# A two-block transformer kernel: six first weight chunks on unnormalised x, w_out's first chunks in three steps, the last sum of squares later

## The chip, the cores and the metric

The kernel runs on one core of a Trainium2 chip. The metric is device time in microseconds (us) of one execution. Five engines take part, each with a queue of its own that it works off in order: TensorE (PE; its weight loads, PEld, overlap the products), VectorE (DVE), ScalarE (ACT), GpSimd (POOL) and SyncE (SP, which issues most transfers). They meet through semaphores alone.

## What is computed

Two blocks in a row on one sequence of 256 tokens and 1024 features. The part that matters here is the first block:

```python
hn = rms_norm(x, ln_g[l])
proj = jnp.einsum('bsd,dc->bsc', hn, w_in[l])
(qa, ka, va, ga, qb, kb, vb, gb, qc, kc, vc, gc, gate_logits) = jnp.split(proj, SPLIT_POINTS, axis=-1)
qa = rms_norm(qa.reshape(b, s, H_A, HEAD_DIM), g[0])
ka = rms_norm(ka.reshape(b, s, H_A, HEAD_DIM), g[1])
o_a = moba_attention(qa, ka, va.reshape(b, s, H_A, HEAD_DIM), rel_bias[OFF_A:OFF_A + H_A])
...
branches = jnp.stack([o_a.reshape(b, s, W_BR) * jax.nn.silu(ga), ...], axis=2)
br = jnp.einsum('bsiw,iwd->bsid', branches, w_branch[l])
merged = jnp.sum(gates * br, axis=2)
x = x + jnp.einsum('bsd,de->bse', merged, w_out[l])
```

The second block has its own norms, modulated by a vector that comes from `silu(c) @ w_ada`, a convolution, attention over selected keys, and a mixture of 64 experts behind a router.

## The kernel before, in words

**Layout and split numbers.** x lies feature by token in eight tiles of 128 features (index k). All products keep float32 accuracy with three products: an operand is split into a rounded high half (H, by a copy on ACT) and the rest (L, a subtraction on DVE), and H·H, H·L and L·H are summed. So a weight chunk of 1024 x 256 costs one transfer of 1 MB, one split on ACT (L249), one on DVE (L250) and 48 products of 256 columns on PE: 8 features x 2 halves x 3.

**The stream of weights.** `L1_ORDER` (L36) lists the chunks of layer 1 by name; w_out's four and the later weights follow. `ahead` (L265) fetches and splits the next chunk, `weight` (L269) hands one out, `early` (L274) calls `ahead` in the middle of a chunk. The five buffers "raw" serve as landing place and for low halves by turns, so chunk n + 3 can land only when PE has done its last product on chunk n's low half.

**The first chunks.** PE first multiplies unnormalised x (times ln_g, halves `xsH`, `xsL`) and the result is scaled by each token's reciprocal norm r when it is read out: `proj_raw` (L670). These raw chunks are 0, 1 and 2 (qa.0, ka.0, va.0). Meanwhile the squares are summed, r is the power -0.5 on POOL (L703), and PE broadcasts r over the partitions into `bc`, a PSUM tile (L708). Then for each feature DVE computes `hn` (L713, reads bc; four buffers), ACT `hH` (L714), DVE `hL` (L715). Those 24 instructions stand in one block in which the orders of ACT and DVE are as written. Chunk 3 (ga.0) and all others use hH and hL.

**The order of the rest.** In layer 1 the order of PE is as written; the other engines' queues are ordered by a planner that takes, of what is ready by its own estimate, what stands first in the program, and so also takes work that is written far behind. `slot` (L446) is called twice in each chunk from chunk 2 on, at its half and its end; `later(d, f)` puts work d slots on. The transposes of qa.0 (`fin`, L757) fall into slot 1, those of ka.0 into slot 3, a chunk's w_ada sum two slots behind it. PSUM has two banks for each name, taken in turn (`pst`, L301): under "O", the sums take the first bank, bc the second, qa.0's transposes the first again and ka.0's the second again.

**w_ada.** `ada_piece` (L609) loads 1/48 of w_ada (0.5 MB, two buffers) and sums its product with silu(c) on DVE (L620). Each chunk from 3 to 50 has one piece; silu(c) itself is computed behind the normalisation (L723 to L728).

**The end of layer 1.** The branch products (L861) make the merged tiles `mg`, two features at a time, with hH (L881) and hL (L882). `proj_fm_k` (L366) multiplies w_out's first two chunks in two steps: features 0 to 5 of both chunks, then 6 and 7. Behind each w_out chunk the new x is squared (`ss_add`, L326), and four small products sum the squares; those of the last chunk stand at the end of layer 1. Layer 2 begins with raw chunks (L1094); behind feature 5, `norm_mod` (L1063) calls `ss_bc` (L338), which computes r by an integer estimate and three rounds of Newton on DVE, in eleven small steps (`rsqrt`, L279), and broadcasts it (L344). `ss_bc` is called a second time ahead of the router.

Of the kernel before, what the change touches and what calls it, by code (L numbers as in the profile page):

```python
# [11 lines left out]
F32 = mybir.dt.float32  # L12
F32R = mybir.dt.float32r
I32 = mybir.dt.int32
AF = mybir.ActivationFunctionType
OP = mybir.AluOpType
# [19 lines left out]
L1_ORDER = """  # L36
qa.0 ka.0 va.0 ga.0 qa.1 ka.1 va.1 ga.1
kvc.0 qc.0 gc.0 qc.1 gc.1
# [33 lines left out]
ROPE_CI, REL_CI = 20, 2  # L72
ATTN_PT, ATTN_PV, ATTN_O, PTS_BUFS = {1: 3, 3: 4}, 2, 1, 6
STOP = False
RAW_BUFS = 5
WARM, START_PARTS = 12, ((0, 2), (2, 4), (4, 8))
RAW_BC, L2_KIWI, TM_K = 6, 0, (4, 6)
ADA_LAG, ADA_SKIP = 2, (0, 1, 2)
L2_LAG = {'qi': 3, 'q': 4, 'k': 3}
# [127 lines left out]
class Build:  # L207
# [70 lines left out]

    def rsqrt(self, src, n, mul, dst, e=None):  # L279
        nc = self.nc  # L280
        e = e or nc.vector
        v = self.tiny.tile([128, 16], F32, tag="rv", name="rv")[:, 0:n]
        y = self.tiny.tile([128, 16], F32, tag="ry", name="ry")[:, 0:n]
        t = self.tiny.tile([128, 16], F32, tag="rt", name="rt")[:, 0:n]
        e.tensor_scalar(v, src, mul, EPS, OP.mult, OP.add)
        e.tensor_scalar(y.bitcast(I32), v.bitcast(I32), -0.5, 0x5F3759DF, OP.mult, OP.add)
        if e is nc.vector:
            for it in range(3):
                o = dst if it == 2 else y
                e.tensor_tensor(t, y, v, OP.mult)  # L290
                e.scalar_tensor_tensor(t, t, -0.5, y, OP.mult, OP.mult)
                e.scalar_tensor_tensor(o, t, 1.5, y, OP.add, OP.mult)
        else:
            for it in range(3):
                o = dst if it == 2 else y
                e.tensor_tensor(t, y, v, OP.mult)
                e.tensor_tensor(t, t, y, OP.mult)
                e.tensor_scalar(t, t, -0.5, 1.5, OP.mult, OP.add)
                e.tensor_tensor(o, t, y, OP.mult)

    def pst(self, shape, tag):  # L301
# [36 lines left out]
    def ss_bc(self, ss):  # L338
        nc = self.nc
        r = self.tiny.tile([128, 4], F32, tag="rr", name="rr")  # L340
        self.rsqrt(ss.rearrange("p a b -> p (a b)"), 4, 1.0 / D, r)
        bc = self.pst([128, S], "O")
        for qt in range(2):
            nc.tensor.matmul(bc[:, 128 * qt:128 * qt + 128], r[:, 2 * qt:2 * qt + 1].to_broadcast([128, 128]),  # L344
                             self.vec("ident"))
        return r, bc
# [19 lines left out]
    def proj_fm_k(self, ws, xs, tags):  # L366

        nc = self.nc
        out = [self.pst([128, 2, S], tag) for tag in tags]
        for ks in (range(KD - 2), (KD - 2, KD - 1)):  # L370
            for ps, (wH, wL) in zip(out, ws):
                for t in range(2):
                    for k in ks:
                        c = k * 256 + 128 * t
                        xH, xL = xs(k)
                        first = k == 0 and t == 0
                        for a, b in ((wH, xH), (wH, xL), (wL, xH)):
                            nc.tensor.matmul(ps[:, t, :], a[:, c:c + 128], b, start=first, stop=k == KD - 1,
                                             skip_group_check=True)
                            first = False  # L380
        return out
# [78 lines left out]
    def attn(self, groups, load_tb, sinks, done):  # L460
# [7 lines left out]
        def qk(g):  # L468
# [24 lines left out]
            if g == G - 1:  # L493
# [4 lines left out]
                else:  # L498
                    self.later(1, lambda: [exps(1), total()])
                for g in range(G):  # L500
                    self.later(ATTN_PT[G] + g, lambda g=g: pt(g))
                    self.later(ATTN_PT[G] + g + ATTN_PV, lambda g=g: pv(g))
                self.later(ATTN_PT[G] + G - 1 + ATTN_PV + ATTN_O, turn)

# [60 lines left out]
    def run(self):  # L565
        tc, nc, a = self.tc, self.nc, self.a
        with ExitStack() as es:
# [25 lines left out]
            with ExitStack() as es1:  # L593
# [4 lines left out]
                with tc.manual_schedule(engines={mybir.EngineType.PE}):  # L598
                    self.layer1()
                if STOP:  # L600
                    return
                self.layer2()
# [20 lines left out]
    def layer1(self):  # L623
        tc, nc, a = self.tc, self.nc, self.a
        x, hH, hL = self.x, self.hH, self.hL
        self.ada_n = 0
        rr = self.s2("rel_a", shape=(128, 512))
        re = self.s2("rel_b", shape=(128, 512))
# [81 lines left out]
        proj_raw(first[1], 4, 8, *w)  # L710
        for k in range(KD):
            hn = self.wk([128, S], "hn", 4)
            nc.vector.scalar_tensor_tensor(hn, x[:, k, :], self.vec("ln_g")[:, k:k + 1], bc, OP.mult, OP.mult)  # L713
            i0 = nc.scalar.activation(hH[:, k, :], hn, AF.Copy)  # L714
            i1 = nc.vector.tensor_tensor(hL[:, k, :], hn, hH[:, k, :], OP.subtract)  # L715
        order.__exit__(None, None, None)
        self.hold = ()
        with tc.issue_after(self.last_load):
            nc.sync.dma_start(self.cmat, a["c_mat"])

        self.silc = self.wk([128, D], "silc", 1)
        th = self.wk([128, D], "ada", ADA_BUFS)
        with tc.issue_after(self.last_load):  # L723
            nc.sync.dma_start(self.silc, bass.AP(a["c_row"].tensor, a["c_row"].offset, [[0, 128], [1, D]]))
        with self.behind((i0.ins,)):
            nc.scalar.activation(th, self.silc, AF.Tanh, scale=0.5)
        with self.behind((i1.ins,)):
            nc.vector.scalar_tensor_tensor(self.silc, th, 1.0, self.silc, OP.add, OP.mult)  # L728
        nsink = self.small([128, 8], F32, "nsink")
        nc.vector.tensor_scalar(nsink, self.vec("sink"), -1.0, None, OP.mult)  # L730
# [55 lines left out]
        def chunk(name, c, ci):  # L786
            if ci < 2:
                self.later(2 * ci + 1, qk_chunk(name, c, first[ci], r))
                return
            wH, wL = self.weight()  # L790
            kind = name[:2]
            if ci == 2:
                ps = self.pst([128, 2, S], "mm")
                T[name, c] = self.s2(name)
                for h in range(2):
                    proj_raw(ps, 4 * h, 4 * h + 4, wH, wL)
                    self.slot()
                for t in range(2):
                    nc.scalar.activation(T[name, c][:, t, :], ps[:, t, :], AF.Copy, scale=r[:, 2 * t:2 * t + 1])
            elif kind in ("va", "vb"):  # L800
                ps = self.proj_tm(wH, wL, self.xs, self.slot)
# [111 lines left out]
        for ci, o in enumerate(L1_ORDER):  # L913
# [15 lines left out]
            if ci not in ADA_SKIP:  # L929
                self.ada_piece()  # L930
            if (name, c) in when:
                self.later(L1_QK if ci > 1 else L1_QK + 1, lambda a=when[name, c]: start(*a))
# [9 lines left out]
        for m in range(4):  # L942
# [7 lines left out]
            self.raw_split(m)  # L950
        while late:
            late.pop(0)()
        self.debug("x1", x.rearrange("p a b -> p (a b)"))
# [129 lines left out]
    def layer2(self):  # L1083
# [8 lines left out]
        raw = [[self.pst([128, S + 2], tag) for t in range(2)] for tag in ("mm", "S", "T")]  # L1092
        for k in range(KD):
            if k == RAW_BC:  # L1094
                h = self.norm_mod(self.ss1)
# [705 lines left out]
```

## Time and profile before

| | us |
|---|---|
| median of 3 runs | 1008.88 (1006.52 to 1009.64) |
| the profiled execution | 1009.1 |
| its span | 1007.1 |
| PE busy | 964.2 (96%) |
| PEld, weight loads | 886.5 (88%) |
| DVE busy | 813.1 (81%) |
| ACT busy | 599.3 (60%) |
| POOL busy | 162.8 (16%) |

The span runs from the first to the last instruction of the profile; 2.0 us of the execution lie around it. Matmuls are pipelined and their ends are modelled, so a busy PE isn't PE at its peak, and the granted clock of PE says how fast it was allowed to run (1.00 is 2.4 GHz, 0.50 is 1.2 GHz). A wait is put down to what released it. Spans on POOL are rough.

### The profile page before, as it was taken

The numbers are of one execution on the slowest core, as the hardware profiler recorded it, in microseconds if no ns is written. First come the engines' busy times: TensorE is split into PE (matmuls) and PEld (weight loads), VectorE is DVE, ScalarE is ACT, GpSimd is POOL, SyncE is SP. The second block draws the span as 40 slices with busy tenths as digits, with TensorE's granted clock in tenths as the row PEclk, the third lists the DMA queues.
The fourth block names the chain that finished last, engine by engine and source line by source line (L and its number), as shares of the span: only waits on it lengthen the run. The fifth ranks groups of instructions, "written<-read, shape, count | busy, mean of one in ns | idle before, by whom it ended". The sixth has DMA issues, their size and how long they took to land. (4 is left out here: it accounts for less than half of the span.)

```text
span 1007.1 us, 20285 instructions
## 1 busy us (share of the span) xinstructions
PE 964.2 (96%) x6666; PEld 886.5 (88%) x6666; DVE 813.1 (81%) x1500; ACT 599.3 (60%) x936; POOL 162.8 (16%) x109
## 2 busy tenths in 40 slices
PE   8799999999999998999989989999999999999996
PEld 7699989999999998999888977788888888888885
DVE  4757877877768668686876689799999999999995
ACT  5455564546545644454544434488787887877874
POOL 2311110111011000030210300012122121221221
PEclk8899999999999999999988989999999999999998
DMA  7366566676566656344331405288888888888984
GB/s 262 139 210 223 207 215 225 251 282 220 198 248 231 233 198 231 131 175 167 129 116 60 161 28 189 74 281 304 300 293 303 286 301 308 293 304 286 308 295 146
DMA packets 51208, 221.91 MB, mean 220 GB/s; under 512 B 5924, under 2 KB 6310, under 8 KB 41552
## 3 DMA queue, kind: packets, MB, share of 16 engines
q1 hardware_dynamic: 48960, 214.67, 60.5%
q0 software_dynamic: 1760, 5.42, 2.2%
q10 hardware_dynamic: 432, 1.05, 0.3%
q8 instruction: 38, 0.62, 0.2%
q14 instruction: 18, 0.15, 0.0%
HBM read 220.01 MB, written 1.11 MB: 220 GB/s over the span
## 5 line engine op out<-in xcount | busy, mean ns | idle before, releaser
L249 ACT ACTIVATE wh<-raw 128x2048 fp32r<-128x2048 f32 x75 | 143.4, 1914 | 110.3 <-DMA raw<-w_in 75.3
L250 DVE TENSOR_TENSOR raw<-raw,wh 128x2048 fp32r<-128x2048 f32 x75 | 171.5, 2287 | 16.2 <-ACT wh L249 15.8
L1542 ACT ACTIVATE wh<-raw 128x1024 fp32r<-128x1024 f32 x136 | 139.3, 1056 | 59.7 <-PE mm L1567 49.6
L350 PE MATMUL mm<-wh,hH 128*128 128x256 f32 x496 | 142.8, 288 | 0.5 <-DVE v L229 0.5
L351 PE MATMUL mm<-raw,hH 128*128 128x256 f32 x496 | 139.6, 281 | 0.2 <-DVE raw L250 0.2
L352 PE MATMUL mm<-wh,hL 128*128 128x256 f32 x496 | 139.6, 281 | 0.0
L1551 POOL TENSOR_TENSOR raw<-raw,wh 128x1024 fp32r<-128x1024 f32 x32 | 76.9, 2404 | 306.2 <-PE mm L1567 306.2
L350 PE MATMUL mm<-hH,wh 128*128 128x256 f32 x352 | 104.3, 296 | 2.0 <-ACT hH L714 2.0
L351 PE MATMUL mm<-hL,wh 128*128 128x256 f32 x352 | 101.3, 288 | 5.0 <-DVE hL L715 4.9
L1566 PE MATMUL mm<-wh,xH 128*128 128x512 f32 x264 | 106.1, 402 | 0.0
L1567 PE MATMUL mm<-wh,xL 128*128 128x512 f32 x264 | 103.4, 392 | 0.0
L352 PE MATMUL mm<-hH,raw 128*128 128x256 f32 x352 | 101.1, 287 | 1.6 <-DVE raw L250 1.6
L350 PEld LDWEIGHTS mm<-wh,hH 128*128 128x128 f32 x496 | 93.6, 189 | 2.2 <-DVE v L229 0.7
L351 PEld LDWEIGHTS mm<-raw,hH 128*128 128x128 f32 x496 | 93.6, 189 | 0.4 <-DVE raw L250 0.4
L352 PEld LDWEIGHTS mm<-wh,hL 128*128 128x128 f32 x496 | 93.6, 189 | 0.1
L620 DVE CUSTOM_DVE_ANT_0 ada<-ada,silc 128x1024 f32<-128x1024 f32 x48 | 58.6, 1221 | 31.8 <-DMA ada<-w_ada 31.6
L1545 DVE TENSOR_TENSOR raw<-raw,wh 128x1024 fp32r<-128x1024 f32 x68 | 79.8, 1210 | 0.0
L1545 DVE TENSOR_TENSOR WL<-raw,wh 128x1024 fp32r<-128x1024 f32 x66 | 79.8, 1210 | 0.0
L351 PEld LDWEIGHTS mm<-hL,wh 128*128 128x128 f32 x352 | 68.9, 196 | 5.8 <-DVE hL L715 5.8
L350 PEld LDWEIGHTS mm<-hH,wh 128*128 128x128 f32 x352 | 68.9, 196 | 3.5 <-ACT hH L714 2.7
L352 PEld LDWEIGHTS mm<-hH,raw 128*128 128x128 f32 x352 | 68.9, 196 | 1.8 <-DVE raw L250 1.8
L427 POOL TENSOR_TENSOR hr<-hss,mhalf 128x8 f32<-128x8 f32 (+2 forms) x24 | 44.2, 1844 | 158.7 <-DVE hss L426 158.5
(515 smaller groups left out, 2539.8 us busy)
## 6 DMA issues: line engine op xcount, KB each, us to landing
raw<-w SPq DMA_DIRECT2D x204, 512.0 KB, 5.3
raw<-w_in SPq DMA_DIRECT2D x58, 1024.0 KB, 4.8
ada<-w_ada SPq DMA_DIRECT2D x48, 512.0 KB, 5.7
raw<-w_out SPq DMA_DIRECT2D x8, 1024.0 KB, 4.8
raw<-w_branch SPq DMA_DIRECT2D x6, 1024.0 KB, 4.8
tb<-rext POOLq DMA_DIRECT2D x20, 256.0 KB, 5.0
raw<-ws SPq DMA_DIRECT2D x3, 1024.0 KB, 5.0
out<-x SPq DMA_DIRECT2D x4, 256.0 KB, 2.3
```

Of the source, the lines that this page charges most:

```text
L249: h = nc.scalar.activation(hi, raw, AF.Copy)
L250: l = nc.vector.tensor_tensor(lo, raw, hi, OP.subtract)
L350: nc.tensor.matmul(out, lh, rh, start=start, stop=False)
L351: nc.tensor.matmul(out, lh, rl, start=False, stop=False)
L352: self.last_mm = nc.tensor.matmul(out, ll, rh, start=False, stop=stop).ins
L427: nc.gpsimd.tensor_tensor(r, ss, self.mhalf[:, 0:2 * nh], OP.pow)
L620: nc.vector.tensor_tensor_reduce(raw, raw, self.silc, 0.5, 0.0, OP.mult, OP.add, self.ada[:, m:m + 1])
L1542: nc.scalar.activation(WH[h][:, half(p)], rw[h][:, half(p)], AF.Copy)
L1545: nc.vector.tensor_tensor(WL[h][:, half(p)], rw[h][:, half(p)], WH[h][:, half(p)], OP.subtract)
L1551: (nc.vector, nc.gpsimd)[f].tensor_tensor(VL[f], rw2[f], VH[f], OP.subtract)
L1566: nc.tensor.matmul(pa, xH[h][:, k, :], WH[h][:, ws], start=h == 0 and k == 0, stop=False)
L1567: nc.tensor.matmul(pa, xL[h][:, k, :], WH[h][:, ws], start=False, stop=False)
```

## The change

The order of the first eight chunks becomes qa.0, ka.0, va.0, qa.1, ka.1, va.1, ga.0, ga.1, and the first six are raw. The normalisation is cut into three pieces (features 0 to 2, 3 to 5, 6 and 7), written behind chunks 2, 3 and 4, without a fixed order of ACT and DVE; silu(c) comes behind chunk 5. The pieces of w_ada begin with chunk 5, and chunks 45 and 48 have two. w_out's first two chunks are multiplied in three steps. The last four sums of squares are written behind the third feature of layer 2's first chunks. `rsqrt` is gone; `ss_bc` computes r by one DVE step and a power on POOL. (The attention's lags move into a variable, with the same values; a switch that was off is removed.)

```diff
-qa.0 ka.0 va.0 ga.0 qa.1 ka.1 va.1 ga.1
+qa.0 ka.0 va.0 qa.1 ka.1 va.1 ga.0 ga.1
...
-ADA_LAG, ADA_SKIP = 2, (0, 1, 2)
+ADA_TWICE = (45, 48)
+ADA_LAG, ADA_SKIP, RAW_CHUNKS = 2, (0, 1, 2, 3, 4), 6
...
     def ss_bc(self, ss):
...
-        self.rsqrt(ss.rearrange("p a b -> p (a b)"), 4, 1.0 / D, r)
+        nc.vector.tensor_scalar(r, ss.rearrange("p a b -> p (a b)"), 1.0 / D, EPS, OP.mult, OP.add)
+        nc.gpsimd.tensor_tensor(r, r, self.mhalf[:, 0:4], OP.pow)
...
-        for ks in (range(KD - 2), (KD - 2, KD - 1)):
+        for ks in (range(4), (4, 5), (6, 7)):
...
-        for k in range(KD):
-            hn = self.wk([128, S], "hn", 4)
-            nc.vector.scalar_tensor_tensor(hn, x[:, k, :], self.vec("ln_g")[:, k:k + 1], bc, OP.mult, OP.mult)
-            i0 = nc.scalar.activation(hH[:, k, :], hn, AF.Copy)
-            i1 = nc.vector.tensor_tensor(hL[:, k, :], hn, hH[:, k, :], OP.subtract)
         order.__exit__(None, None, None)
...
+        def normalize(k0, k1):
+            for k in range(k0, k1):
+                hn = self.wk([128, S], "hn", 4)
+                nc.vector.scalar_tensor_tensor(hn, x[:, k, :], self.vec("ln_g")[:, k:k + 1], bc, OP.mult, OP.mult)
+                nc.scalar.activation(hH[:, k, :], hn, AF.Copy)
+                nc.vector.tensor_tensor(hL[:, k, :], hn, hH[:, k, :], OP.subtract)
+
+        def condition():
+            self.silc = self.wk([128, D], "silc", 1)
+            th = self.wk([128, D], "ada", ADA_BUFS)
+            with tc.issue_after(self.last_load):
+                nc.sync.dma_start(self.silc, bass.AP(a["c_row"].tensor, a["c_row"].offset, [[0, 128], [1, D]]))
             nc.scalar.activation(th, self.silc, AF.Tanh, scale=0.5)
             nc.vector.scalar_tensor_tensor(self.silc, th, 1.0, self.silc, OP.add, OP.mult)
+
+        between = {2: lambda: normalize(0, 3), 3: lambda: normalize(3, 6), 4: lambda: normalize(6, KD), 5: condition}
...
         def chunk(name, c, ci):
-            if ci < 2:
-                self.later(2 * ci + 1, qk_chunk(name, c, first[ci], r))
+            if ci < RAW_CHUNKS:
+                if ci < 2:
+                    ps = first[ci]
+                else:
+                    wH, wL = self.weight()
+                    ps = self.pst([128, 2, S], "mm")
+                    for h in range(2):
+                        proj_raw(ps, 4 * h, 4 * h + 4, wH, wL)
+                        self.early(h)
+                        self.slot()
+                if name[0] == "v":
+                    T[name, c] = self.s2(name)
+                    for t in range(2):
+                        nc.scalar.activation(T[name, c][:, t, :], ps[:, t, :], AF.Copy, scale=r[:, 2 * t:2 * t + 1])
+                else:
+                    self.later(2 * ci + 1 if ci < 2 else L1_LAG[name[0]], qk_chunk(name, c, ps, r))
+                if ci in between:
+                    between[ci]()
                 return
...
             if ci not in ADA_SKIP:
                 self.ada_piece()
+            if ci in ADA_TWICE:
+                self.ada_piece()
...
-        while late:
-            late.pop(0)()
+        self.late = late
...
         for k in range(KD):
+            if k == 3:
+                while self.late:
+                    self.late.pop(0)()
             if k == RAW_BC:
                 h = self.norm_mod(self.ss1)
```

## Rows read from the trace of the kernel before

**Rows 1.** The page, part 1: busy time and share of the span of each engine.
```profile
PE 964.2 (96%) x6666; PEld 886.5 (88%) x6666; DVE 813.1 (81%) x1500; ACT 599.3 (60%) x936; POOL 162.8 (16%) x109
```

**Rows 2.** Stretches: length, busy (count) by engine, TensorE clock, DMA share, GB/s.
```profile
40.00:50.00 10.00, 5.47 (x19) 4.10 (x20) 7.03 (x11) 4.00 (x5) 0.00 (x0) 0.63 0.37 128
...
60.00:70.00 10.00, 10.00 (x87) 9.59 (x84) 8.18 (x18) 6.11 (x14) 2.38 (x2) 1.00 0.79 279
```

**Rows 3.** Waits of PE, 35 to 60 us: total, times, longest.
```profile
PE mm L351 <- DVE hL L715: 4.9, 2, 3.1
PE mm L350 <- ACT hH L714: 2.0, 2, 1.6
```

**Rows 4.** Timeline of PE, 29 to 62 us: start, length, instruction, idle before.
```profile
29.65 0.39 PE L681 MATMUL mm<-wh,xsH 128*128 128x256 f32 x1
...
35.44 0.60 PE L436 MATMUL O<-vecs,qn 128*128 128x128 f32 x4
35.79 0.37 PE L350 MATMUL mm<-hH,wh 128*128 128x256 f32 x1
...
53.24 0.60 PE L436 MATMUL O<-vecs,qn 128*128 128x128 f32 x4
```

**Rows 5.** Timeline of DVE, 20 to 75 us.
```profile
26.16 0.48 DVE L713 SCALAR_TENSOR_TENSOR hn<-x,vecs,O 128x256 f32<-128x256 f32 x1 [3.43 <-PE O L708]
...
33.22 2.29 DVE L250 TENSOR_TENSOR raw<-raw,wh 128x2048 fp32r<-128x2048 f32 x1
...
37.41 0.69 DVE L752 TENSOR_TENSOR qn<-qn,hr 128x512 f32<-128x512 f32 x1 [1.17 <-POOL hr L427]
...
46.32 0.48 DVE L713 SCALAR_TENSOR_TENSOR hn<-x,vecs,O 128x256 f32<-128x256 f32 x1
47.28 0.42 DVE L715 TENSOR_TENSOR hL<-hn,hH 128x256 fp32r<-128x256 f32 x1 [0.48 <-ACT hH L714]
```

**Rows 6.** Timeline of SP, which issues the fetches, 20 to 75 us.
```profile
28.98 6.97 SPq L241 DMA_DIRECT2D raw<-w_in  x2
```

**Rows 7.** DMA issues, 20 to 70 us: count, size, median us to landing.
```profile
raw<-w_in SPq DMA_DIRECT2D x5, 1024.0 KB, 4.8
```

**Rows 8.** The page, part 5: busy us, mean ns of one, idle before.
```profile
L249 ACT ACTIVATE wh<-raw 128x2048 fp32r<-128x2048 f32 x75 | 143.4, 1914 | 110.3 <-DMA raw<-w_in 75.3
```

**Rows 9.** Timeline of DVE, 385 to 405 us.
```profile
391.46 1.22 DVE L620 CUSTOM_DVE_ANT_0 ada<-ada,silc 128x1024 f32<-128x1024 f32 x1
...
397.81 2.29 DVE L250 TENSOR_TENSOR raw<-raw,wh 128x2048 fp32r<-128x2048 f32 x1
400.01 1.29 DVE L882 TENSOR_TENSOR hL<-mg,hH 128x512 fp32r<-128x512 f32 x2
```

**Rows 10.** Timeline of PE, 395.5 to 405 us.
```profile
396.84 0.36 PE L378 MATMUL mm<-hH,wh 128*128 128x256 f32 x1 [0.37 <-DVE gate L877]
...
400.75 0.39 PE L378 MATMUL mm<-hL,wh 128*128 128x256 f32 x1 [2.11 <-DVE hL L882]
```

**Rows 11.** Stretches of 2 us, 390 to 450 us.
```profile
402.00:404.00 2.00, 2.00 (x11) 2.00 (x11) 1.87 (x4) 1.87 (x2) 0.00 (x0) 0.50 0.03 8
```

**Rows 12.** Timeline of PE, 427 to 438 us.
```profile
430.33 0.50 PE L334 MATMUL O<-ones,sqx 128*128 128x2 f32 x4
...
435.77 0.61 PE L344 MATMUL O<-vecs,rr 128*128 128x128 f32 x4
```

**Rows 13.** Timeline of DVE, 568 to 607 us.
```profile
580.70 0.16 DVE L285 TENSOR_SCALAR rv<-O 128x4 f32<-128x4 f32 x1 [1.04 <-PE O L334]
...
582.87 0.48 DVE L1330 SCALAR_TENSOR_TENSOR r<-O,rr,lrow 128x64 f32<-128x64 f32 x2
```

**Rows 14.** Timeline of POOL, whole span.
```profile
33.41 3.97 POOL L427 TENSOR_TENSOR hr<-hss,mhalf 128x8 f32<-128x8 f32 x1 [1.45 <-DVE hss L426]
...
92.93 1.12 POOL L427 TENSOR_TENSOR hr<-hss,mhalf 128x4 f32<-128x4 f32 x1 [3.39 <-DVE hss L426]
```

**Rows 15.** Waits of PE, 430 to 1007 us.
```profile
PE mm L350 <- DVE v L229: 0.5, 1, 0.5
```

More of the change, by code (lines that the diff above doesn't have):

```diff
@@ L72 @@
 ROPE_CI, REL_CI = 20, 2
-ATTN_PT, ATTN_PV, ATTN_O, PTS_BUFS = {1: 3, 3: 4}, 2, 1, 6
-STOP = False
+L1_ATTN, PTS_BUFS = ({1: 3, 3: 4}, 2, 1), 6
+ADA_TWICE = (45, 48)
 RAW_BUFS = 5
@@ L277, in early @@
             self.ahead()
[L279 to L299, printed above, removed]
     def pst(self, shape, tag):
@@ L499, in qk @@
                     self.later(1, lambda: [exps(1), total()])
+                d_pt, d_pv, d_o = self.lags
                 for g in range(G):
-                    self.later(ATTN_PT[G] + g, lambda g=g: pt(g))
-                    self.later(ATTN_PT[G] + g + ATTN_PV, lambda g=g: pv(g))
-                self.later(ATTN_PT[G] + G - 1 + ATTN_PV + ATTN_O, turn)
+                    self.later(d_pt[G] + g, lambda g=g: pt(g))
+                    self.later(d_pt[G] + g + d_pv, lambda g=g: pv(g))
+                self.later(d_pt[G] + G - 1 + d_pv + d_o, turn)
         def exps(half):
@@ L599, in run @@
                     self.layer1()
-                if STOP:
-                    return
                 self.layer2()
@@ L626, in layer1 @@
         self.ada_n = 0
+        self.lags = L1_ATTN
         rr = self.s2("rel_a", shape=(128, 512))
@@ L710, in layer1 @@
         proj_raw(first[1], 4, 8, *w)
-        for k in range(KD):
-            hn = self.wk([128, S], "hn", 4)
-            nc.vector.scalar_tensor_tensor(hn, x[:, k, :], self.vec("ln_g")[:, k:k + 1], bc, OP.mult, OP.mult)
-            i0 = nc.scalar.activation(hH[:, k, :], hn, AF.Copy)
-            i1 = nc.vector.tensor_tensor(hL[:, k, :], hn, hH[:, k, :], OP.subtract)
         order.__exit__(None, None, None)
-        self.hold = ()
         with tc.issue_after(self.last_load):
             nc.sync.dma_start(self.cmat, a["c_mat"])
[L721 to L725, printed above, removed]
+        def normalize(k0, k1):
[9 more added lines that the diff above has]
+                nc.sync.dma_start(self.silc, bass.AP(a["c_row"].tensor, a["c_row"].offset, [[0, 128], [1, D]]))
             nc.scalar.activation(th, self.silc, AF.Tanh, scale=0.5)
-        with self.behind((i1.ins,)):
             nc.vector.scalar_tensor_tensor(self.silc, th, 1.0, self.silc, OP.add, OP.mult)
+        between = {2: lambda: normalize(0, 3), 3: lambda: normalize(3, 6), 4: lambda: normalize(6, KD), 5: condition}
         nsink = self.small([128, 8], F32, "nsink")
@@ L791, in chunk @@
             kind = name[:2]
[L792 to L800, printed above, removed]
+            if kind in ("va", "vb"):
                 ps = self.proj_tm(wH, wL, self.xs, self.slot)
```

## The prediction

> **What bounds the kernel now.** I read the page's first part: PE is busy for 964.2 us, 96% of the span, and the next engine, DVE, 81% [rows 1]. So an edit counts by the PE idle time or slow PE clock that it removes, and must not make DVE, the next engine, late. The table of stretches shows where PE loses. From 60 to 70 us it is busy for all 10.00 us at clock 1.00 with DVE at 8.18; from 40 to 50 it is busy for 5.47 us, at a granted clock of 0.63, with DVE at 7.03 [rows 2]. The list of waits for 35 to 60 us names the cause: PE waits 4.9 us for hL and 2.0 us for hH, the two halves of normalised x [rows 3]. The timeline of PE shows the price: chunk 2 (va.0), on unnormalised x, runs from 29.65 to 35.44, 5.79 us for 48 products; chunk 3 (ga.0), the first on normalised x, also 48 products, runs from 35.79 to 53.24, 17.45 us [rows 4]. Of that 6.9 us are waits; the rest of the excess, 17.45 - 5.79 - 6.9 = 4.8 us, goes with the half clock behind them. DVE shows why hL is late: the first hn starts at 26.16, the eighth only at 46.32, since hn, hH and hL follow each other in an order by hand, with splits of weights of 2.29 us and a scaling that waits 1.17 us for POOL between them [rows 5].
>
> **Part 1: six raw chunks.** Chunks 3 to 5 (qa.1, ka.1, va.1) become raw and ga.0, ga.1 become chunks 6 and 7. No product is added: a raw chunk has 48, as a normalised one. Chunk 3 would cost what chunk 2 does, so the removed loss is 17.45 - 5.79 = 11.66 us [rows 4], if nothing new stops PE in the 23 us of chunks 2 to 5. What could:
> - Weights. SP's queue fetches chunk n+3 when PE ends chunk n: the two issues merged from 28.98 to 35.95 stand at the ends of chunks 1 and 2 [rows 6]. A fetch lands in 4.8 us [rows 7], the split takes 1.9 us on ACT [rows 8] and 2.3 on DVE, together 9.0 us; the chunks between take 2 x 5.79 = 11.6. So 2.6 us of cover: nothing, while ACT and DVE are prompt. If that cover is gone, PE waits for the excess.
> - DVE. From 26.16 to 53 it has four splits (9.2), normalisation 8 x (0.48 + 0.42) = 7.2, four scalings with their reductions (about 1.5 each, 6), silc 1.2 and first score sums (1.2): 25 of 27 us by durations, some 2 us less by the spacing of their starts. It is nearly full, but PE needs hH and hL only in chunk 6, near 53.5.
> - The bank of bc. The reciprocal norm broadcast lies in the second O bank, and the transposes of ka.0 (slot 3, now the end of chunk 3, near 41.5) take the same bank. So PE there waits until all eight hn have read bc, though normalize(6, 8) stands behind chunk 4 in the program. The hn are free to run from 26.16 on, with holes in DVE in front of 26.16 and of the waits for POOL [rows 5]; no hand-made order now puts ACT between them. Eight hn, the hL that free their four buffers, two splits and two scalings are some 13 us, ready near 39 to 42. I take 0.6 us of PE wait; bounds 0 and 4 (as late as 45.5).
> - The scaling of raw q and k by r is two ACT passes for one, and va.1's two scaled copies replace one copy: under 1 us of ACT, which was busy 60% [rows 1]; 0.
> - silc's load, tanh and product move behind chunk 5, in SP's queue behind the fetch of chunk 7. It needs no buffer that is late, so what is queued behind it (the first w_ada piece, the next fetch) is delayed by its issue of some 0.4 us only; who waits for silc is the sum of that piece, and behind it DVE's next splits. Under the 2.6 us cover: 0. Its earlier place at the start gives nothing back, because PE waits there for x and its splits.
>
> **Part 2: w_ada.** Two pieces leave the start (free) and come back at chunks 45 and 48. Each is one 0.5 MB load and a DVE sum of 1.22 us. The second load's buffer is free only after an earlier sum, so SP holds the next fetch for a moment; those fetches are 5.8 us apart: 0. The second pair's sum falls due where DVE has no hole before w_out: at 391.46 a sum, at 397.81 a split, at 400.01 the hL of features 2 to 5 [rows 9]. I take +0.6 us, bounds 0 and +1.3 (nothing hidden).
>
> **Part 3: three steps in w_out.** PE starts w_out at 396.84, does six products (features 0 and 1), and waits 2.11 us, to 400.75, for an hL [rows 10]; behind that the clock is 0.50 [rows 11]. The stalled product is the eighth, feature 2. The new first step still takes features 0 to 3, so the same wait stands in it, and the features 4 and 5 that it puts off are there 0.6 us later in any case. 0; the bound below is -3.5 (the 2.11 and, an estimate, 1.4 for three us at half clock), if DVE puts hL ahead of the split of 397.81; above nothing, since the second chunk's weights, now needed 12 products sooner, are split by 400.1.
>
> **Part 4: sums later.** The last four products of squares already run at 430.33, inside layer 2, and the broadcast of r only at 435.77, with PE busy between [rows 12]. Putting them behind feature 2 leaves them about there: 0, bounds -0.3 and +1.
>
> **Part 5: power on POOL.** Twice, eleven small DVE steps become one and a power of 128x4 on POOL. At the router the chain from the sums to r's first user takes 582.87 - 580.70 = 2.17 us [rows 13], and the router's later steps on PE hang on it. The same power on 128x4 took 1.12 us; one of 128x8, started 0.19 us behind a split on DVE, took 3.97 [rows 14]. With a hand-over of about 0.4 the new chain is 1.5 or 4.3: -0.6 or +2.1; nearest is the first, since the DVE steps of that chain follow each other with no split between them; I take -0.3, as other DVE work lies between. In layer 2's start 5.4 us lie between sums and broadcast [rows 12]: 0 to +1, taken 0. The Trainium skill (SBUF — State Buffer, section Who interferes with whom) says that a GpSimd instruction that reads SBUF and a DVE instruction with two SBUF inputs share one port pair, and whichever issues second is fully blocked. The 3.97 agrees. By that rule, if a split starts first, this part is +2.1 and the sum about -8.4.
>
> **Part 6, unspoken:** va.1 no longer calls the copy that alternates between ACT and DVE, so every later alternating copy changes engine. The number on each stays even; PE's longest wait for one is 0.5 us [rows 15]. 0, bounds -2 and +2 over some tens of copies.
>
> **Sum.** -11.66 + 0.6 + 0.6 + 0 + 0 - 0.3 = -10.8 us. The profiled execution took 1009.1 us (2.0 around the span); the median of the runs shown is 1008.88, 0.2 below. Forecast 1009.1 - 10.8 = 998.3.
>
> **Rivals.**
> - A, DVE becomes the bound of chunks 3 to 6: its list is 25 of 27 us, and in-order waits for POOL (1.17 us in [rows 5]) recur four times. PE then waits some 3 us in pieces, and the clock may fall: -11.66 + 3 + 2 + 0.3 = -6.4, 1002.7. Against it: 60 to 70 us, with attention on top, no PE gap at DVE 8.18 [rows 2]. 0.2.
> - B, the w_out stall goes too: -10.8 - 3.5 = -14.3, 994.8. For: one exchange of two DVE instructions does it, and the added sum changes what is ready when; against: the program order of both is unchanged. 0.15.
> - C, slower: the bank wait of slot 3. If the last hn stays as late as now, behind the splits of chunks 3 to 5 and one more, PE stands from 41.5 until S later and pays again the 4.8 us of slow clock. It decides at S = 11.66 - 4.8 = 6.9 us, the eighth hn at 48.4; at 46.32, its present time [rows 5], the kernel still wins 2 us. One more split in front (2.2) gives 48.5, and with the tail's 0.3 about 1009.5; waiting also for chunk 3's own scaling gives 1012. 0.05.
> - D, nothing to be measured: the same wait with S near 5 to 6, or the same loss moved to chunk 6, 1006 to 1008. 0.05.
> - E, the power meets a split at the router, by the mechanism of [rows 14]: 998.3 + 2.4 = 1000.7. 0.1, the single contended price against 1.12.
> The forecast itself: 0.45, from 996 to 1000.5.
>
> **Numbers.** 0.3% (3 us) is about what a measurement of this kernel can tell from no change. The forecast, A, B and E are faster by more than that: 0.9; D with part of C 0.06; slower 0.04. The range from 994.3 to 1003.2 takes in forecast, E, B's value and A's value with the unknown ends of the copies; left out are C, D and B's and A's far halves.
>
> **What would show it.** Right: PE busy without gap from 29.65 to about 60 at clock 1.00, the transposes of ka.0 near 41.5, the eighth hn before them; ga.0 a chunk of 5.8 us; qa.1 ended near 41.3 instead of 59.3; w_out's start some 11 us sooner with its wait still on feature 2's hL; the power 1.1 us at the router. Wrong: a wait of those transposes on an hn (C, D); PE waits for raw or hL in chunks 4 to 6 (A); w_out begun and run without a wait (B); PE idle in new places behind 60 us, which the moved copies or the earlier second half of attention a would have made.

## The result, and the profile after

The changed kernel takes 998.7 us (median of 5 runs, 996.76 to 1000.53), the kernel before, timed beside it, 1009.64 us (5 runs, 1006.52 to 1013.48): ratio 0.989, 95% interval 0.986 to 0.992. Forecast were 998.3, with a range of 994.3 to 1003.2. The total came out as forecast; two of its terms did not, each by some 3 us, and in opposite directions. The profiled execution of the changed kernel took 997.92 us, its span 996.0 (before: 1009.1 and 1007.1).

The table cuts both traces at the same instructions of PE; a stage is the time from one start to the next, read from PE's timeline. The last stage ends with PE's last product, 5.8 us before the end of either span.

| stage, by PE's instructions | before, us | after, us | difference | forecast |
|---|---|---|---|---|
| start to the first transposes (end of chunk 2) | 35.44 | 32.94 | -2.50 | 0 |
| to the next transposes (chunk 3) | 17.80 | 7.65 | -10.15 | -11.1 |
| to the first scores of branch c | 64.22 | 65.07 | +0.85 | 0 |
| to the first product of w_out | 279.38 | 281.27 | +1.89 | +0.6 |
| to the first sums of squares in w_out | 17.04 | 13.78 | -3.26 | 0 |
| to layer 2's first products with kiwi (a tile of 72 columns of its weights) | 34.51 | 34.70 | +0.19 | 0 |
| to layer 2's first attention scores | 67.64 | 66.99 | -0.65 | 0 |
| to the products of the router weights | 35.89 | 37.28 | +1.39 | 0 |
| to the second sums of squares | 10.41 | 10.60 | +0.19 | 0 |
| to the first product of the routing | 29.44 | 29.95 | +0.51 | -0.3 |
| to the end | 409.60 | 409.98 | +0.38 | 0 |

The first chunks. The page's busy times of the changed kernel (they answer to [rows 1]), and its stretches beside [rows 2] (length, busy and count of PE, PEld, DVE, ACT and POOL, clock, DMA share, GB/s):

```profile
PE 960.5 (96%) x6666; PEld 884.2 (89%) x6666; DVE 809.0 (81%) x1479; ACT 599.9 (60%) x940; POOL 162.2 (16%) x111
```

```profile
40.00:50.00 10.00, 9.41 (x79) 9.15 (x80) 7.21 (x13) 7.13 (x11) 1.66 (x1) 1.00 0.54 181
60.00:70.00 10.00, 10.00 (x87) 9.67 (x86) 7.83 (x19) 5.88 (x11) 0.72 (x1) 1.00 0.64 224
```

From 40 to 50 us PE is now busy for 9.41 us at clock 1.00, where it was 5.47 at 0.63. PE's timeline (start, length, instruction, idle before it and who ended that), beside [rows 4], and the one wait that PE has between 25 and 70 us, in place of [rows 3]:

```profile
27.16 0.39 PE L660 MATMUL mm<-wh,xsH 128*128 128x256 f32 x1
...
32.94 0.60 PE L415 MATMUL O<-vecs,qn 128*128 128x128 f32 x4
33.30 0.36 PE L660 MATMUL mm<-wh,xsH 128*128 128x256 f32 x1
...
40.59 0.63 PE L415 MATMUL O<-vecs,qn 128*128 128x128 f32 x4 [1.36 <-DVE hn L697]
```

```profile
PE O L415 <- DVE hn L697: 1.4, 1, 1.4
```

Chunk 3 (qa.1, raw) runs from 33.30 to 40.59 - 1.36 = 39.23, 5.93 us for the 17.45 of ga.0 before. The wait behind it is the one that the prediction set at 0.6: ka.0's transposes need the bank that the last hn reads. DVE's timeline, beside [rows 5], says why it is late:

```profile
25.05 0.47 DVE L697 SCALAR_TENSOR_TENSOR hn<-x,vecs,O 128x256 f32<-128x256 f32 x1
...
36.43 2.28 DVE L250 TENSOR_TENSOR raw<-raw,wh 128x2048 fp32r<-128x2048 f32 x1
38.63 1.42 DVE L699 TENSOR_TENSOR hL<-hn,hH 128x256 fp32r<-128x256 f32 x4
39.97 0.47 DVE L697 SCALAR_TENSOR_TENSOR hn<-x,vecs,O 128x256 f32<-128x256 f32 x1
```

The eighth hn starts at 39.97 instead of 46.32, behind a split and the four hL that free its buffer.

w_out, PE's timeline beside [rows 10] and DVE's beside [rows 9]:

```profile
386.93 0.36 PE L357 MATMUL mm<-hH,wh 128*128 128x256 f32 x1 [0.84 <-DVE gate L867]
...
388.20 0.39 PE L357 MATMUL mm<-hH,wh 128*128 128x256 f32 x1 [0.32 <-ACT hH L871]
388.92 0.38 PE L357 MATMUL mm<-hL,wh 128*128 128x256 f32 x1 [0.34 <-DVE hL L872]
```

```profile
388.18 0.69 DVE L872 TENSOR_TENSOR hL<-mg,hH 128x512 fp32r<-128x512 f32 x1 [0.20 <-ACT hH L871]
388.79 2.28 DVE L250 TENSOR_TENSOR raw<-raw,wh 128x2048 fp32r<-128x2048 f32 x1
390.99 0.68 DVE L872 TENSOR_TENSOR hL<-mg,hH 128x512 fp32r<-128x512 f32 x1
```

The 2.11 us of [rows 10] have become 0.34. On DVE the hL of features 2 and 3 now stands ahead of a split behind which it stood before; the hL of features 4 and 5 still follows the split.

### The profile page after: what moved, and what is told of

The parts are those of the page before. It is cut to its first block, busy times and chain, and to the rows that moved or that the text cites. A ratio compares the mean times of both kernels' runs of the same rounds, so it can differ in the third digit from the quotient of the medians.

```text
span 996.0 us, 20282 instructions
## 1 busy us (share of the span) xinstructions
PE 960.5 (96%) x6666; PEld 884.2 (89%) x6666; DVE 809.0 (81%) x1479; ACT 599.9 (60%) x940; POOL 162.2 (16%) x111
## 5 line engine op out<-in xcount | busy, mean ns | idle before, releaser
L329 PE MATMUL mm<-wh,hH 128*128 128x256 f32 x448 | 128.5, 287 | 0.0
L331 PE MATMUL mm<-wh,hL 128*128 128x256 f32 x448 | 125.9, 281 | 0.0
L330 PE MATMUL mm<-raw,hH 128*128 128x256 f32 x448 | 125.8, 281 | 0.0
L329 PEld LDWEIGHTS mm<-wh,hH 128*128 128x128 f32 x448 | 84.5, 189 | 1.5
L330 PEld LDWEIGHTS mm<-raw,hH 128*128 128x128 f32 x448 | 84.5, 189 | 0.2 <-DVE raw L250 0.2
L331 PEld LDWEIGHTS mm<-wh,hL 128*128 128x128 f32 x448 | 84.4, 188 | 0.1
L406 POOL TENSOR_TENSOR hr<-hss,mhalf 128x8 f32<-128x8 f32 (+2 forms) x24 | 41.8, 1743 | 169.0 <-DVE hss L405 168.8
L331 PEld LDWEIGHTS mm<-hH,raw 128*128 128x128 f32 x352 | 66.9, 190 | 1.2 <-DVE raw L250 1.2
```

What stands on the lines that cost most here:

```text
L329: nc.tensor.matmul(out, lh, rh, start=start, stop=False)
L330: nc.tensor.matmul(out, lh, rl, start=False, stop=False)
L331: self.last_mm = nc.tensor.matmul(out, ll, rh, start=False, stop=stop).ins
L406: nc.gpsimd.tensor_tensor(r, ss, self.mhalf[:, 0:2 * nh], OP.pow)
```

## The experiments

Twelve further runs were timed in three groups of four, each group beside the kernel before, whose median there lay between 1008.17 and 1009.32 us. Each ratio is to the kernel before of the run's own group. Theory at the outset: the first chunks bring 10 us, and w_out's wait went because an edit further up turned DVE's order round. Rival: the three steps took that wait away by themselves.

**w_out: which edit took the wait.** First the changed kernel with two steps, and the kernel before with three:

```
-        for ks in (range(4), (4, 5), (6, 7)):
+        for ks in (range(KD - 2), (KD - 2, KD - 1)):
```

> The changed kernel with its first w_out chunks back in two steps (features 0 to 5, then 6 and 7). Theory (an earlier edit turned the order on VectorE round: hL of features 2 and 3 now stands ahead of the split at 388.79, and the three steps only keep PE from asking for features 4 and 5 too soon): PE asks for feature 4 about 2.1 us after it had feature 2, while its hL ends at 391.67, so one wait of 1.5 to 2.5 us for hL at feature 4, none over 0.5 at feature 2; from the start of w_out to its first sums 15.5 to 17 us instead of 13.8, the time 1000 to 1002. Rival (the three steps alone took the old wait away): the old wait of 2.1 us for hL at feature 2 is back with the half clock behind it, 17.0 us, the time 1001 to 1002. Third (steps don't matter at all): 13.8 us, 998.7.

> The kernel before with the three steps alone. Theory (the wait in w_out is set by VectorE's order, which this edit leaves as it was): the wait of about 2.1 us for hL at feature 2 and the half clock behind it stay, from the start of w_out to its first sums 16.5 to 17.1 us as in the kernel before (17.04), the time within 0.1% of the kernel before. Rival (the three steps are what took the wait away in the changed kernel): the wait falls below 0.5 us, 13.8 us, the time 3 us (0.3%) lower.

Measured with two steps: 1000.63 us, ratio 0.991 (0.988 to 0.994); w_out takes 17.42 us. Three steps alone in the kernel before: 1007.62 us, 0.999 (0.996 to 1.001); 17.08 us. PE's timeline of the first, then of the second, at w_out:

```profile
390.24 0.38 PE L357 MATMUL mm<-hL,wh 128*128 128x256 f32 x1 [0.34 <-DVE hL L872]
...
393.04 0.39 PE L357 MATMUL mm<-hL,wh 128*128 128x256 f32 x1 [1.83 <-DVE hL L872]
```

```profile
399.12 0.38 PE L378 MATMUL mm<-hL,wh 128*128 128x256 f32 x1 [2.03 <-DVE hL L882]
```

The theory holds in both, though w_out took more than its 15.5 to 17 us with two steps. There feature 2 is there in time, and PE stops at feature 4 instead; with three steps in the old order it stops at feature 2 as before. A wait of 1.83 us cost 17.42 - 13.78 = 3.64, since the clock fell behind it, as in [rows 11]; a stretch of that kernel:

```profile
395.00:397.00 2.00, 2.00 (x12) 2.00 (x11) 2.00 (x2) 0.00 (x0) 0.00 (x0) 0.50 0.00 0
```

Next, what turned the order. One kernel sets it by hand in the kernel before, one takes the doubled pieces of ada out of the changed kernel, and one puts these pieces and the three steps alone into the kernel before:

```
+        with self.behind((self.hl1,) if len(self.todo) == HOLD else ()):   # h_order: kernel before, with three steps
+            l = nc.vector.tensor_tensor(lo, raw, hi, OP.subtract)
...
-ADA_TWICE = (45, 48)                                                       # k_ada_end: changed kernel
+ADA_TWICE = ()
...
-ADA_LAG, ADA_SKIP = 2, (0, 1, 2)                                           # m_twice: kernel before, with three steps
+ADA_LAG, ADA_SKIP = 2, (0, 1, 2, 3, 4)
+ADA_TWICE = (45, 48)
...
+            if ci in ADA_TWICE:
+                self.ada_piece()
```

> The kernel before with the three steps, and VectorE's half of the split of w_out's second chunk held behind hL of features 2 and 3. Theory (order on VectorE and steps remove the wait only together; the first chunks are not needed for it): hL of features 2 and 3 comes some 1.6 us sooner, its wait falls from 2.1 to 0.5 us or less, no half clock follows, from the start of w_out to its first sums 13.8 to 15 us instead of 17.0, the time 2 to 3.2 us (0.2 to 0.3%) under the kernel before. Rival (the held split is late next: PE asks for w_out's second chunk 4.1 us after the first): the wait moves there with 1 to 2 us and its half clock, 16 to 17 us, no gain.

> The changed kernel without the two doubled pieces of ada: the last two pieces come behind the last chunk. Theory (the doubled pieces turned VectorE's order in w_out: without them the split stands ahead of hL of features 2 and 3 again): the wait of about 2 us for hL at feature 2 and the half clock are back in spite of the three steps, 16.5 to 17.5 us from the start of w_out to its first sums instead of 13.8, the time 2 to 4 us over the changed kernel's. Rival (the doubled pieces only cost their 1.2 us each on VectorE ahead of w_out): w_out stays at 13.8 us, the time 0 to 1 us lower.

> The kernel before with the three steps and the doubled pieces of ada (and the two later starts that pay for them), its first chunks as they were. Theory (these two small edits together are all of w_out's gain): from the start of w_out to its first sums 13.6 to 14.4 us instead of 17.0, the time 2.5 to 3.3 us (0.25 to 0.33%) under the kernel before. Rival (the first chunks are needed as well): 16.5 us or more, no gain.

Measured: order by hand 1006.72 us, 0.999 (0.997 to 1.000), w_out 14.40 us with waits of 0.49 and 0.49. Without the doubled pieces 1001.41 us, 0.993 (0.992 to 0.995), w_out 17.20 us. Doubled pieces and steps in the kernel before 1006.77 us, 0.998 (0.997 to 1.000), w_out 13.25 us. The totals of the first and last lie 1.5 and 1.6 us under the kernel before, less than the 2 to 3.3 that were expected and under the 0.3% that can be told; the stage is plain. The total without the doubled pieces is: 2.5 us above the changed kernel timed in the same group (1001.14 to 1003.18 against 996.83 to 1000.47). DVE and PE without the doubled pieces, then DVE with them in the kernel before:

```profile
388.65 2.28 DVE L250 TENSOR_TENSOR raw<-raw,wh 128x2048 fp32r<-128x2048 f32 x1
390.85 1.29 DVE L872 TENSOR_TENSOR hL<-mg,hH 128x512 fp32r<-128x512 f32 x2
```

```profile
391.59 0.39 PE L357 MATMUL mm<-hL,wh 128*128 128x256 f32 x1 [2.27 <-DVE hL L872]
```

```profile
396.68 0.69 DVE L883 TENSOR_TENSOR hL<-mg,hH 128x512 fp32r<-128x512 f32 x1
397.29 2.28 DVE L251 TENSOR_TENSOR raw<-raw,wh 128x2048 fp32r<-128x2048 f32 x1
```

The two doubled pieces, put in for another reason, changed what stands ahead of what on DVE, though no line about hL or the split was touched. Order and steps together take 2.6 to 3.8 us from this stage (14.40 and 13.25 for 17.04; 3.26 in the changed kernel), and neither does so alone; the first chunks are not needed for it.

**The first chunks.** One kernel frees the bank of the broadcast at once, one makes only four chunks raw, one puts parts 3 to 5 into the kernel before without the first chunks, and the changed kernel runs again:

```
+        bs = self.wk([128, S], "bs", 1)                       # d_bank: hn reads bs instead of bc
+        nc.scalar.activation(bs, bc, AF.Copy)
...
-RAW_CHUNKS = 6                                                # i_raw4
+RAW_CHUNKS = 4
-        between = {2: lambda: normalize(0, 3), 3: lambda: normalize(3, 6), 4: lambda: normalize(6, KD), 5: condition}
+        between = {2: lambda: normalize(0, 4), 3: rest}       # rest: normalize(4, KD), then condition()
```

> The changed kernel with the broadcast reciprocal copied by ScalarE into SBUF, from where the eight products read it, so that its PSUM bank comes free at once. Theory (the 1.36 us wait of ka.0's transposes for the last hn is the bank's): the wait is gone, ka.0's transposes come at 39.2 to 39.5 us instead of 40.6, the time 1.0 to 1.4 us lower than the changed kernel's. Rival (VectorE is what is short in chunks 3 to 6): the wait moves to ka.0's own normalisation or to hL of ga.0 and the time stays within 0.3 us.

> The changed kernel with four first chunks on unnormalised x instead of six; all eight features are formed behind the third and fourth. Theory (the price of a chunk that asks for the eighth hL before VectorE has it is that wait alone): ka.1 reaches feature 7 about 2.5 us after its start near 41 and the eighth hL ends at 44.7, so one wait of 1 to 1.5 us, the time 1 to 2.5 us over the changed kernel's. Rival (VectorE falls behind for good, as in the kernel before): waits of 3 us or more and a clock of 0.5 behind them, 4 us or more. Third (six are more than is needed): no wait, the same time.

> The kernel before with the three steps, the later sums and the power on POOL, but its first chunks, their order and the gates as they were. Theory (the first chunks carry the gain, by the early wait and by the order on VectorE that follows from them): the time 0 to 1.5 us below the kernel before, w_out's wait still there, layer 2's start and router no shorter end to end. Rival (the three parts behind the first one are worth some 3 us by themselves): ratio 0.997 or lower.

> The changed kernel once more, beside the three above. Theory (the stretch in which PE's clock is halved at the start falls now here, now there, in either kernel): its first chunk ends anywhere between 26.3 and 28.9 us, the wait of ka.0's transposes is the shorter the later PE comes (1.36 at 26.4, 0.6 at 28.3), w_out takes 13.8 us again, the time 996 to 1000. Rival (the earlier start belongs to the change): 26.4 us again.

The free bank: 998.11 us, 0.988 (0.985 to 0.992). The wait is gone and chunk 3's stage takes 6.12 us for 7.65, but w_out starts 353.97 us behind the first transposes, as in the changed kernel (386.93 - 32.94 = 353.99). The theory has the wait right and the time not shown: PE's waits in the attention between differ by as much from trace to trace (one of 1.2 us for a gated result stands here and in the run with two steps, and not in the changed kernel, whose code is the same up to there as with two steps).

Four raw chunks: 1003.18 us, 0.994 (0.990 to 0.997). PE's waits and a stretch of it:

```profile
PE mm L329 <- ACT hH L698: 2.0, 1, 2.0
PE mm L331 <- DVE hL L699: 1.1, 1, 1.1
```

```profile
50.00:60.00 10.00, 10.00 (x76) 9.63 (x74) 6.95 (x15) 5.80 (x13) 3.37 (x3) 0.87 0.48 184
```

The rival is nearer: the waits come to 3.2 us instead of 1 to 1.5, and the clock falls behind them. The fifth and sixth raw chunk together are worth some 3 to 5 us (ratio 0.994 against the changed kernel's 0.989 and 0.990 of the other groups); the five runs lie far apart, from 995.57 to 1006.14.

Parts 3 to 5 without the first chunks: 1011.22 us, 1.001 (1.000 to 1.003). They bring nothing. The theory had them 0 to 1.5 us below the kernel before, and w_out's wait and the later stages as they came; the median is 1.9 us above, and 3.6 us above the three steps alone in the same group (1011.22 and 1007.62, twelve runs each), to which the part on three nanoseconds comes back.

The changed kernel again: 998.87 us, 0.990 (0.989 to 0.992), its chunk 1 ends at 27.25 us. Over all traces that end lies between 26.3 and 28.9, in either kernel: 28.88, 26.72, 28.73, 26.31 and 27.42 with the old chunks; 26.39, 26.64, 27.37, 28.34, 27.17, 28.67, 27.11, 27.25 and 27.44 with the new. So the 2.50 us of the table's first line are chance: a stretch of low clock lay at 20 us in the profiled execution of the kernel before, and at 8 us, between two waits of PE for its first weights (2.00 and 0.65 us), in that of the changed kernel. First of before, then of after:

```profile
20.00:22.00 2.00, 2.00 (x10) 2.00 (x10) 1.67 (x2) 0.00 (x0) 1.35 (x1) 0.50 0.18 74
```

```profile
8.00:10.00 2.00, 2.00 (x12) 2.00 (x10) 0.65 (x3) 1.06 (x3) 0.00 (x0) 0.50 1.07 419
```

The bank's wait shrinks by what PE comes later: with six raw chunks and the bank not freed it is 1.4 us in the two traces with chunk 1 ended by 26.64, and 0.6 us in the four from 27.11 to 28.34.

**Copies and roots.** One kernel turns the alternating copies back, one puts the two late roots back on DVE:

```
                 if name[0] == "v":
                     T[name, c] = self.s2(name)
+                    self.flip ^= c                            # e_parity
...
-        nc.vector.tensor_scalar(r, ss.rearrange("p a b -> p (a b)"), 1.0 / D, EPS, OP.mult, OP.add)
-        nc.gpsimd.tensor_tensor(r, r, self.mhalf[:, 0:4], OP.pow)
+        self.rsqrt(ss.rearrange("p a b -> p (a b)"), 4, 1.0 / D, r)     # g_root
```

> The changed kernel with the alternating copy flipped once more at va.1, so that every later alternating copy is on the engine that it had before. Theory (part 6 is worth nothing): every stage within 1 us of the changed kernel's, the time within 0.2%. Rival (the turned copies cost at the end of layer 2, where the changed kernel takes 37.1 to 37.3 us from the first scores to the router weights against 35.9 in the kernel before): that stage falls by 1 to 1.4 us and the time with it.

> The changed kernel with the reciprocal roots of the two late norms back on VectorE. Theory (the power makes the broadcast at the router 1.0 us sooner, but what follows waits for something else): from the second sums to the broadcast 20.8 us instead of 19.8, from there to the routing products 8.7 instead of 10.2, the sum 29.4 to 29.5 instead of 29.95; at layer 2's start within 0.2 us; the time 0 to 0.5 us lower. Rival (the sooner broadcast is worth its 1.0 us): the sum 31 us and the time 1 us higher.

Copies turned back: 996.87 us, 0.988 (0.986 to 0.990); not to be told from the changed kernel's 0.989 and 0.990. Inside, one wait follows the copies: PE's wait for ACT's tanh of a gate, 1.7 us in the changed kernel, is 0.5 again (waits from 105 to 388 us; first the changed kernel, then this one). It is 0.4 to 0.8 in all seven kernels whose copies alternate as in the kernel before and 1.6 to 2.1 in the seven others. The stage from layer 2's scores to the router weights takes 35.88 us, but it lies between 35.9 and 37.4 in traces of either sort, so its part is open. Not every stage stayed within 1 us, as the theory had it: w_out took 15.26 us, with the clock low from 390 to 394 us behind the same waits as in the changed kernel.

```profile
PE mm L329 <- ACT gate L809: 1.7, 1, 1.7
```

```profile
PE mm L329 <- ACT gate L810: 0.5, 1, 0.5
```

Roots on DVE: 996.79 us, 0.989 (0.987 to 0.991). From the second sums to the routing it takes 29.42 us (20.80 + 8.62) instead of 29.95, as the theory has it; at layer 2's start 35.71 instead of 34.70, which it does not have: with the sums moved, the eleven DVE steps are late there by 1.0 us, and the power is what keeps part 4 free. Why the sooner broadcast at the router wins nothing: POOL and DVE of the changed kernel,

```profile
568.98 1.04 POOL L320 TENSOR_TENSOR rr<-rr,mhalf 128x4 f32<-128x4 f32 x1 [8.17 <-DVE rr L319]
```

```profile
568.73 0.16 DVE L319 TENSOR_SCALAR rr<-O 128x4 f32<-128x4 f32 x1 [1.06 <-PE O L312]
570.05 0.48 DVE L1324 SCALAR_TENSOR_TENSOR r<-O,rr,lrow 128x64 f32<-128x64 f32 x2 [1.16 <-POOL rr L320]
...
577.98 0.75 DVE L1308 SCALAR_TENSOR_TENSOR raw<-T,rr,wh 128x512 fp32r<-128x512 f32 x1 [1.70 <-ACT wh L1307]
```

and the last of these with the roots on DVE:

```profile
577.11 0.75 DVE L1351 SCALAR_TENSOR_TENSOR raw<-T,rr,wh 128x512 fp32r<-128x512 f32 x1 [0.35 <-ACT wh L1350]
```

The power took 1.04 us and the chain 570.05 - 568.73 = 1.32 us for the 2.17 of [rows 13]. Behind it DVE's queue waits 1.70 us instead of 0.35 for ACT's half of a transposed feature, ahead of the top-k. ACT in turn waits for PE's transposes, and these come 1.0 us later with the power, although the broadcast that stands ahead of them on PE comes sooner (570.07 instead of 570.74). First the changed kernel, then the roots on DVE:

```profile
572.63 1.04 PE L1303 MATMUL T<-vecs,xf 128*128 128x128 f32 x8
```

```profile
571.66 1.03 PE L1346 MATMUL T<-vecs,xf 128*128 128x128 f32 x8
```

PE multiplies without a gap in between, so what became later is the transposes' place among other products of layer 2.

**Three nanoseconds per product.** Two roots on DVE cost 1.0 us at one place and gave 0.5 at the other, yet the kernel was not slower (ratio 0.989, beside 0.989 and 0.990); these totals alone cannot tell a difference of that size. The traces can, in the products whose moving operand is hH or hL (gates, w_out and the like in layer 2: 3 x 352 of them by the page's groups). The same chunk of gates, 48 products with two transposes among them, from its first product to the first of the next chunk, at clock 1.00 and without a wait, in four kernels in this order: before, the kernel before with parts 3 to 5, changed, changed with roots on DVE:

```profile
379.32 0.36 PE L350 MATMUL mm<-hH,wh 128*128 128x256 f32 x1
...
385.01 0.28 PE L350 MATMUL mm<-bH,wh 128*128 128x256 f32 x1
```

```profile
379.56 0.36 PE L351 MATMUL mm<-hH,wh 128*128 128x256 f32 x1
...
385.40 0.28 PE L351 MATMUL mm<-bH,wh 128*128 128x256 f32 x1
```

```profile
368.75 0.36 PE L329 MATMUL mm<-hH,wh 128*128 128x256 f32 x1
...
374.60 0.28 PE L329 MATMUL mm<-bH,wh 128*128 128x256 f32 x1
```

```profile
369.03 0.36 PE L372 MATMUL mm<-hH,wh 128*128 128x256 f32 x1
...
374.72 0.28 PE L372 MATMUL mm<-bH,wh 128*128 128x256 f32 x1
```

5.69, 5.84, 5.85 and 5.69 us. From start to start of neighbouring products of this form (gaps over 150 ns left out, some 1000 in each trace) the mean is 116.9 to 117.0 ns in the six kernels that have the DVE root anywhere (before, b_three_steps, h_order, m_twice, g_root, j_best) and 119.8 to 119.9 in the eight that have not. It is so in every stretch of the run (116.7 to 117.3, and 119.7 to 120.3), long before a root is computed. The products in which hH is the stationary operand take the same in all (118.1 to 118.4 ns). What the two sorts differ in up to there is, by their code, memory alone: the root's scratch tiles (rv, ry, rt, three buffers of 64 bytes each) are 576 bytes per partition, and what is allocated behind them, the weight chunks among it, lies that much lower without them, while hH and hL, allocated ahead, stay. 3.0 ns x 1056 products = 3.2 us, an estimate. The table bears out its larger part: from the end of chunk 3 to w_out both kernels run at clock 1.00 and PE idles as long (5.72 and 5.81 us), but it is busy for 2.65 us more, against 2.4 to 2.6 us by 3.0 ns for each product of the 17 (before) or 18 (after) such chunks that lie there. First before, then after:

```profile
53.24:396.84 343.60, 337.88 (x2872) 330.45 (x2871) 253.16 (x507) 182.94 (x322) 40.16 (x34) 1.00 0.64 229
```

```profile
40.59:386.93 346.34, 340.53 (x2871) 332.66 (x2871) 258.47 (x512) 185.62 (x328) 40.03 (x34) 1.00 0.64 230
```

In the same stretch of the other traces that have no low clock in it PE is busy for 337.6 and 337.9 us with the tiles (m_twice, j_best) and for 340.0 to 340.7 without (c_first, a_two_steps, d_bank, e_parity, k_ada_end). That the tiles' presence goes with the spacing is shown in 14 traces of 14; that the place of the weights against hH is the cause is argued, and was not tried by itself.

**Together.** The changed kernel with the bank freed, the copies turned back, the power at layer 2's start and the DVE root at the router:

```
+        if ss is self.ss1:
             nc.vector.tensor_scalar(r, ss.rearrange("p a b -> p (a b)"), 1.0 / D, EPS, OP.mult, OP.add)
             nc.gpsimd.tensor_tensor(r, r, self.mhalf[:, 0:4], OP.pow)
+        else:
+            self.rsqrt(ss.rearrange("p a b -> p (a b)"), 4, 1.0 / D, r)
```

> The changed kernel with the broadcast reciprocal copied to SBUF, the copy flipped at va.1 and the router's root back on VectorE, the power kept at layer 2's start. Theory (the three small prices add): the transposes' wait of 0.6 to 1.4 us gone, second sums to routing products 29.4 instead of 29.95, first scores of layer 2 to the router weights 35.9 instead of 36.1 to 37.3, layer 2's start as in the changed kernel (34.7 from sums to the index keys' products): 0.8 to 2 us below the changed kernel. Rival (what is won before w_out is taken back by the attention's waits, as in the run with the copy alone): 0.5 us or nothing.

Measured: 992.77 us (990.06 to 994.24), ratio 0.984 (0.982 to 0.986), 6.1 us below the changed kernel of the same group (996.83 to 1000.47; no run of one lies among those of the other; 3.7 between the two profiled executions). That is three times the theory's upper end, which knew nothing of the 3.2 us of the scratch tiles; with them its terms come to 4.0 to 5.2. One of these terms did not come: the stage to the router weights took 37.36 us, not 35.9. This version beats both kernels. Page, busy times:

```profile
PE 955.2 (96%) x6666; PEld 878.5 (89%) x6666; DVE 811.2 (82%) x1490; ACT 598.6 (60%) x940; POOL 161.9 (16%) x110
```

## Why the prediction was right, and where it was wrong

- **Part 1, six raw chunks**: right in mechanism and size. Chunk 3 fell to 5.93 us, the bank's wait came where it was said, with 1.36 or 0.6 us for the 0.6 taken, no half clock followed it, PE had no other gap to 70 us. The chunk's stage gave 10.15 of the 11.06 forecast. That wait for an hn stands among the prediction's own signs of being wrong; it was too short for that. Rival A did not occur: DVE, at 7 to 8.5 us in 10, kept up. Rival C was far off: the last hn came at 39.97, the point of decision was 48.4.
- **Part 2, w_ada**: +0.6 priced its 1.22 us of DVE. What it did was to change DVE's order, and with part 3 that was worth -3.3.
- **Part 3, three steps**: the step that failed is "the same wait stands in it", with the reason given against rival B, "the program order of both is unchanged". Program order did not settle it: the hL passed the split, the very exchange that part 3's lower bound names, for -3.5, and rival B, held at 0.15, is what happened in w_out (-3.26). It did not carry the total to B's 994.8, because of part 5.
- **Part 4, sums later**: 0, right; but only with the power beside it (1.0 us late without).
- **Part 5, power**: the power's 1.04 us and a chain of 1.32 were as forecast (1.12 and 1.5). "-0.3" failed twice. At the router the stage became 0.51 longer, since DVE waits next for ACT and ACT for transposes that PE reaches later; and the step that the prediction did not have at all is what went with the removed tiles: +3.2 us over 1056 products. Rival E did not occur: no split ran beside the power. The Trainium skill's rule on the shared port (SBUF — State Buffer, section Who interferes with whom) was not put to the test there, since DVE stood idle while POOL worked.
- **Part 6, copies**: 0 for the total cannot be told from what was measured. One wait for a gate grew from 0.5 to 1.7 us, between 105 and 388 us, a stretch that [rows 15], from 430 us on, do not cover; PE's idle time from chunk 3 to w_out stayed at 5.7 to 5.8 us all the same.

So the forecast of -10.8 met -10.9 (medians 998.7 and 1009.64; -9.5 in the last group) by two errors of about 3 us that cancel, -3.3 in w_out and +3.2 in the products; that they cancel is luck. In the table, -2.50 at the start is chance, chunk 3 and w_out give -13.4, and the other lines add up to +4.75. Of this, 2.74 in the two stages between chunk 3 and w_out is the products' spacing, and 0.51 the router. The 1.39 ahead of the router weights goes with a granted clock of 0.86 over that stage instead of 0.90, and the stage takes as long in kernels of either sort; the remaining four lines add up to 0.1.

## What to carry to other kernels

Where an engine's order comes out of a scheduler, an edit that adds work to it can move two untouched instructions past each other: look at the order on the engine, not at the program, before writing "the same wait stands". If two waits stand behind each other, price the edits together, since either alone may be worth nothing. And when a kernel is slower or faster than its parts, compare the same instruction's spacing in a stretch that no edit touches.

## What was not expected of the hardware

- The spacing of products with hH or hL moving is 116.9 ns in kernels with 576 bytes more of scratch and 119.9 in those without, 2.6% at the same clock of 1.00; products of the same size with hH stationary show no difference (118.1 to 118.4 ns in all).
- A wait of PE of 1.36 to 1.4 us at 40 us left the clock at 1.00 (changed kernel, 30 to 50 us), one of 1.83 to 2.27 in w_out was followed by 0.50. But the run with the copies turned back has a clock of 0.55 from 390 to 392 us behind waits of 0.84, 0.32 and 0.34, and w_out took 15.26 us there; in the changed kernel the same three waits left it at 1.00. The waits before it alone do not settle it.
